# Background jobs of the opening feed-forward group of a hybrid encoder layer: weight sums begun two blocks earlier, both jobs stepped in each cell of the down-projections

## The chip, the cores and the metric

The kernel runs on one core of one Trainium2 chip. It is written with its own instruction order on TensorE, ScalarE, VectorE and GpSimd (in the feed-forward part the program text is the order); the order of SyncE's queue, which issues most of the transfers, is set by a scheduler. The metric is the time of one execution on the device, in microseconds. A profile of one execution gives the busy time of each engine (PE is TensorE's matrix multiplication, PEld its weight loads, DVE is VectorE, ACT is ScalarE, POOL is GpSimd, SP is SyncE), what each instruction waited for, and when each transfer landed.

## The reference, cut to what matters

One inference step of one layer, over 2048 prompt tokens and 64 sample tokens (2112 together), model width 1024, feed-forward width 2816. The first half of the layer (modulated norm, input projection, pooling mixer beside an mLSTM, output projection) isn't touched by the change. The second half is:

```python
    x = x + gt1 * mix
    h2 = rmsnorm(x, g2) * (1 + sc2) + sh2
    up = h2 @ w_up                                    # 1024 -> 2 * 2816
    upp = jnp.concatenate([conv_buf.astype(up.dtype), up], 1)
    conv = b_conv + sum(w_conv[j] * upp[:, j:j + T] for j in range(CONV_W))   # causal, width 3
    a, g = jnp.split(conv, 2, -1)
    x = x + gt2 * ((jax.nn.silu(g) * a) @ w_down)     # 2816 -> 1024
    ...
    y = rmsnorm(x, g_final)
```

All of it is float32.

## The kernel before, in words

**Arithmetic.** A float32 operand is split into a rounded high part and the low rest, and every product of the reference is computed as three matrix multiplications of such parts (`PASSES`). Splitting a weight tile takes a rounding on ScalarE (L411) and a subtraction on VectorE (L414).

**Groups, blocks, parts.** The 2112 tokens of the feed-forward part are done in three groups of 704 (`FT`; its half, 352, is `FH`). In each group the width 2816 is done in 22 blocks of 128 + 128 columns of `w_up` (one half for `a`, one for `g`). A block, `Pair.products`, multiplies the normed input of the group with its columns by a fast scheme of seven products in place of eight; each product (`product`, L1586) is 12 matmuls of 128 x 128 by 128 x 352. One of the seven, named T4, is not done in its own block but in the middle of the next one (`last_product`). The right-hand operands of the products are seven sums of chunks of the normed input, named B11, B21, B22, T1, T2, T3, T4; they come ready from the device's memory (`Bd`) and are held in SBUF as `hx`. Between its products a block steps along the convolution and the gate of the block before and the one before that. The result of a block is kept as `av` (a pool with 7 buffers, `AVB`).

In group 0 the 22 blocks come in four parts: 0 to 4, 5 to 9, 10 to 15 and 16 to 21. Behind each part stands the down-projection of what the part has made: for each of the 8 rows n of 128 output columns (`KD`) and each block k of the part one *cell*, which multiplies an `av` with a weight tile for two ranges of tokens (448 and 256 wide, `ENDS`): 2 x 3 matmuls. With five blocks in a part that is 40 cells, with six 48. At a row's end VectorE adds its two PSUM banks to `x3`, the residual (`rows_add`, L2009). There are six banks, two to a row. The rows 0 to 2 are begun early and ended together, since the last blocks of a part are not ready at first; what the last block still has to do (its T4 product, the sums, the convolution, the gate) lies in a list `todo`, whose steps are taken one behind each cell. In groups 1 and 2 the first parts are done by another scheme (`quad_down`), which needs sums of the down-projection's weights.

**Background jobs.** Two jobs of group 0 make what group 1 needs. They are Python generators, and a call of `tick(i)` carries job i on by one `yield`, that is by one instruction or none, so the place of a call sets the instruction's place in the order of its engine.

Job 0 is `quad_sums` (L1643): the sums of the down-projection's weights. For each of 16 pieces it takes a buffer of the `av` pool (the tile is named `qs`), loads the piece on SyncE's queue (L1649), makes four subtractions or additions on VectorE (L1653 to L1659) and stores the piece to `dsum` on SyncE's queue (L1662). A piece has 13 yields, the job 208.

Job 1 is `prepare` (L818): the seven sums of group 1's normed input. After a broadcast of the norms' factors it does four chunks; each loads two rows of the residual (`x2d`) into two scratch tiles `fscr` (L828, SyncE's queue), rescales them (`normed`, L737 on VectorE and L740 on ScalarE), and makes the seven sums from them, each with its high part (ScalarE, L788), its low part (VectorE, L774) and a store to `Bd` (L840, ScalarE's queue), between which VectorE makes the next difference (L770). The scratch pool has four buffers. The job has about 91 yields. When it has ended, a `reload` (L1872) loads the seven sums back into `hx`, on SyncE's queue, stepped by `tick(1)` too.

Calls of `tick` stand in these places: `product` makes two `tick(0)`, so a block with seven products makes 14; `products` makes four `tick(1)` (L1729, L1740, L1743, L1746); a cell of a down-projection does a step of `todo` if there is one, and else one `tick`, of job 1 or job 0 by turns (L2171). Job 0 gets `quad_sums` when the blocks of part 0 are done (L2137), job 1 gets `prepare` at the same place. Ahead of the last down-projection of the group whatever is left of both is run out at once (`drain`, L2140).

**Weights.** The tiles of `w_up` and `w_down` come as a stream: `pump` (L421) is called ahead of each product and behind each cell; it issues the loads on SyncE's queue, a few tiles ahead, into 5 raw buffers, and splits those next in line into 7 split buffers, so that the place of `pump` in the text sets where the splits stand in ScalarE's and VectorE's order.

The steps that the prediction speaks of are so on these engines: SyncE (loads of weights, of `x2d` and of the pieces, stores of pieces, reloads), ScalarE (roundings L411 and L788, the stores of `Bd`), VectorE (L414, L737, L770, L774, L1653 to L1659, L2009), TensorE (products L1594, cells L2160).

Of the kernel before, what the change touches and what calls it, by code (L numbers as in the profile page):

```python
# [64 lines left out]
def tile_layer(ctx: ExitStack, tc: tile.TileContext, xT, vecs, cst, rst, w_mod, w_ada, w_qkou, w_v, w_pool,  # L65
# [38 lines left out]
    bg = ([], [], [], [], [])  # L104

    def tick(i=0):
        q = bg[i]
        while q:
            try:
                next(q[0])  # L110
                return
            except StopIteration:
                q.pop(0)
# [143 lines left out]
    for g in range(NG):  # L257
        o = Grp()
# [400 lines left out]
    for g in range(NFG):  # L659
        o = Grp()  # L660
# [878 lines left out]
    def do(n=1):  # L1539

        for _ in range(n):
            if todo:
                todo.pop(0)()
# [91 lines left out]
    def give(bk):  # L1635
        used.remove(bk)
        free.append(bk)
# [49 lines left out]
    class Pair:  # L1687
# [10 lines left out]
        def products(self, old):  # L1698


            o, Bo, f = self.o, self.Bo, self.f
            self.before = old
            older = old and old.before
            if older and older.ended:
                older = None
            open_ = old and not old.shut

            def rest(*steps):
                for pair, step in steps:
                    if pair:  # L1710
                        step(pair)
            b1 = self.b1 = take()
            product(b1, Bo, "B11", True)
            if open_:
                old.sum_g1()
                old.sum_a()
            rest((older, Pair.gate))
            b2 = self.b2 = take(True)
            seed(b2, b1)
            rest((older, Pair.step_2))  # L1720
            b3 = self.b3 = take()
            product(b3, Bo, "T1", True)
            self.s5 = half_tile("s5")
            act.activation(self.s5, b3.t[:, :FH], AF.Copy)
            rest((old, Pair.scale_a), (older, Pair.step_3))
            if open_:
                old.last_product()
            rest((old, Pair.taps_a), (older, Pair.step_4))
            tick(1)  # L1729
            product(b1, Bo, "T2", False)  # L1730
            seed(b3, b1)
            if open_:
                old.sum_g0()
            rest((old, Pair.scale_g))
            self.ea = ext_tile(o, f, "a")
            product(b2, Bo, "B21", False)
            copied(o, 0, self.ea, b2)
            give(b2)
            rest((older, Pair.step_5), (old, Pair.taps_g))
            tick(1)  # L1740
            product(b1, Bo, "B22", False)
            rest((old, Pair.silu), (older, Pair.step_6))
            tick(1)  # L1743
            product(b3, Bo, "T3", False)
            rest((older, Pair.step_7))
            tick(1)  # L1746
            if older:
                older.ended = True

# [361 lines left out]
    for o in fgroups:  # L2111
        Bo = B[o.g]
        held = None
        for pi, part in enumerate(PARTS[o.g]):
            f0, f1_ = part
            nf = f1_ - f0
            lastp = pi == len(PARTS[o.g]) - 1
            ends = o.last and lastp
            av = [None] * nf
            quad = Quad() if paired(o.g, part) else None  # L2120
            if pi == 0:
                pair = None
            for f in range(f0, f1_):
                old, pair = pair, Pair(o, Bo, f, f - f0, av, quad)
                pair.products(old)
                if o.g == 0 and len(x3) < KD or pi == 0 and not bg[0]:
                    x3 += load_x2(o, range(len(x3), min(len(x3) + 2, KD)))
                if held is not None:
                    quad_down(o, held, pair, old)
                    held = None  # L2130
            if pi == 0 and o.g > 0:
                drain(0)
                x3 += load_x2(o, range(len(x3), KD))
            if not o.last:
                if pi == 0:
                    if o.g == 0:
                        bg[0].append(quad_sums())  # L2137
                    bg[1].append(prepare(fgroups[o.g + 1], fscr))
                if lastp:
                    drain(0, 1)  # L2140
                    B.append(Sums())
                    bg[1].append(reload(B[-1]))
            if lastp:
                ssum = fscr("ssum")
            if quad is not None:
                held = quad
                continue

            def down(bks, W, ks, secs, stays=False, plain=False):

                cells = [(i, k) for i in range(len(secs)) for k in ks]
                if plain:
                    cells.sort(key=lambda c: c[1])
                for c, (i, k) in enumerate(cells):
                    U = W.at(k // 4)
                    lo, hi = secs[i]
                    if k == 0:
                        bks[i].start(hi - lo)
                    for (a, b) in PASSES:
                        pe.matmul(bks[i].t[:, :hi - lo], U[:, a, k % 4 * P:(k % 4 + 1) * P], av[k][:, b, lo:hi],  # L2160
                                  start=(k == 0 and (a, b) == PASSES[0]), stop=(k == nf - 1 and (a, b) == PASSES[-1]))
                    if (k % 4 == 3 or k == nf - 1) and not stays and i == len(secs) - 1:
                        live[0] -= 1
                    if c % len(secs):
                        continue
                    pump()
                    settle()
                    if todo:
                        do()
                    else:  # L2170
                        tick(1 - c // len(secs) % 2)  # L2171

            def down_end(n, bks, secs):
                for bk, (lo, hi) in zip(bks, secs):
                    rows_add(o, n, lo, hi, bk)
                    give(bk)
                if not lastp:
                    return
                lo, hi = secs[0][0], secs[-1][1]
                if ends and n == KD - 1:  # L2180
                    sq7 = fscr()
                    for (a, b, s) in o.segs:
                        a, b = max(a, lo), min(b, hi)
                        if a < b:
                            act.activation(sq7[:, a - lo:b - lo], x3[n][:, a:b], AF.Square)
                    sums.append((sq7, lo))
                else:
                    fsq_acc(ssum, x3[n][:, lo:hi], lo, hi, n == 0)
                if ends:
                    act.activation(x3[n][:, lo:hi], x3[n][:, lo:hi], AF.Copy, scale=V[:, V_GF + n:V_GF + n + 1])  # L2190

            Ws = [Row() for _ in range(NE)]
            bks = []

            old = pair.before
            todo.extend([both_of(pair.sum_g1, old.gate), both_of(pair.sum_a, old.split_hi), both_of(old.split_lo, pair.scale_a)])
            for n in range(NE - 1):
                bks.append([take() for _ in ENDS])
                down(bks[n], Ws[n], range(nf - 2), ENDS, plain=n == 0)
                if n == 0:  # L2200
                    do(9)
                    pair.last_product()
                    todo.extend([both_of(pair.sum_g0, pair.scale_g), pair.taps_a, pair.taps_g, pair.silu, pair.gate,
                                 pair.split_hi, pair.split_lo])
            for n in range(NE - 1):
                down(bks[n], Ws[n], [nf - 2], ENDS)
            bks.append([take() for _ in ENDS])
            down(bks[-1], Ws[-1], range(nf - 1), ENDS)
            do(9)
            for n in range(NE):  # L2210
                down(bks[n], Ws[n], [nf - 1], ENDS)
                down_end(n, bks[n], ENDS)
            rows = {n: Row() for n in range(NE, KD)}
            for secs in [(c,) for c in ENDS] if ends else (ENDS,):
                sums = [(ssum, 0)]
                for n in range(NE, KD):
                    ps = [take() for _ in secs]
                    down(ps, rows[n], range(nf), secs, ends)
                    down_end(n, ps, secs)
                if ends:  # L2220
                    bg[0].append(final_end(o, x3, sums, *secs[0]))
            pair = None
        if not o.last:
            drain(1)
            bg[0].append(final(o, x3, ssum))
            x3 = []
# [87 lines left out]
```

## Time and profile before

| what | value |
|---|---|
| time, median of 3 runs | 2173.13 us (2171.32 to 2175.94) |
| the profiled execution: its own time, its span | 2174.68 us, 2172.9 us |
| TensorE's granted clock in it | 0.998 |
| TensorE, matmuls | 2151.4 us, 99% of the span |
| VectorE | 1634.9 us, 75% |
| ScalarE | 1096.1 us, 50% |
| GpSimd | 258.4 us, 12% |
| transfers | 539.51 MB, 248 GB/s in the mean |
| group 0: blocks 0 to 4, down-projection of part 0 | to 858.45 us, to 899.34 us |
| part 1: blocks 5 to 9, its down-projection | to 967.70 us, to 1005.67 us |
| part 2: blocks 10 to 15, its down-projection | to 1088.0 us, to 1132.2 us |
| part 3: blocks 16 to 21, its down-projection | to 1213.9 us, to 1257.8 us |

How to read it: the span is the time from the first instruction to the last as the profiler saw it, and the execution's own time has a little around it. The busy times of the engines overlap each other; an engine that is 99% busy leaves room for a change of 1% at most, where it alone is looked at. Times in windows and timelines are counted from the start of the span. A row of a timeline has the time at which an instruction begins, how long it took, the engine, the line of the kernel, the operation, the tile that is written and those that are read, their shapes, and in brackets how long the engine had stood idle before and what ended that. A row of a window has its bounds, its length, the busy time and the number of instructions of PE, PEld, DVE, ACT and POOL, the granted clock, the busy share of the DMA engines, and GB/s.

### The profile page before, as it was taken

To read this page: it belongs to the slowest core of one execution; us is meant where nothing else is said; L and a number is where in the kernel's file an instruction comes from. 1 tells how busy PE (TensorE), PEld (TensorE's weight loads), DVE (VectorE), ACT (ScalarE), POOL (GpSimd) and SP (SyncE) were. 2 spreads that over 40 slices of the span, in tenths; PEclk is the share of its full clock that TensorE was granted. 3 is DMA by queue.
4 is the path that set the end of the run, shared out by engine and by line. 5 is a ranking of instruction groups with operands and counts; after the bars stand their busy time and mean duration, and the time that the engine had idled before them with its cause. 6 is when DMAs were issued, how large, how long until landed. Compare 5 with 4: busy or idle time off the path is not lost.

```text
span 2172.9 us, 38060 instructions
## 1 busy us (share of the span) xinstructions
PE 2151.4 (99%) x13553; PEld 2044.4 (94%) x13553; DVE 1634.9 (75%) x3040; ACT 1096.1 (50%) x2181; POOL 258.4 (12%) x475
## 2 busy tenths in 40 slices
PE   8999999999999999999999999999999999999998
PEld 7888888888899999999999999999999999999998
DVE  5878668667955778797967668888886597887874
ACT  4554335334333446464736445655655365565554
POOL 0010000001000201010101220100101321111112
PEclk9999999999999999999999999999999999999999
DMA  8987997987888477888967976666668675555542
GB/s 319 328 305 233 323 321 246 309 302 244 301 283 288 169 260 239 282 292 300 350 214 255 321 245 222 234 208 209 228 222 274 223 255 186 170 177 190 171 160 77
DMA packets 297351, 539.51 MB, mean 248 GB/s; under 512 B 25760, under 2 KB 114336, under 8 KB 297160
## 3 DMA queue, kind: packets, MB, share of 16 engines
q1 hardware_dynamic: 286568, 511.87, 69.6%
q10 hardware_dynamic: 10592, 25.20, 3.0%
q8 instruction: 107, 1.75, 0.3%
q14 instruction: 84, 0.69, 0.1%
HBM read 410.98 MB, written 125.98 MB: 247 GB/s over the span
## 4 chain that ended last, share of the span: by engine, by line
PE 85%; DMA 5%; DVE 5%; issue 2%; ACT 2%; SPq 0%; POOL 0%; DVEq 0%; ACTq 0%; POOLq 0%
PE mm L1594 34%; PE mm L478 22%; PE mm L2160 12%; PE mm L2037 8%; PE mm L1133 3%; DVE wt L414 1%; DMA wt<-wsum 1%; PE m L1323 1%; DMA hl_kept<-wt 1%; PE m L1308 1%; PE m L1343 1%; PE m L1345 1%; DVE tg L1572 1%; DMA raw<-w_qkou 0%; ACT wt L411 0%
## 5 line engine op out<-in xcount | busy, mean ns | idle before, releaser
L1594 PE MATMUL mm<-hx,wt 128*128 128x352 f32 x5544 | 885.9, 321 | 0.7 <-DVE wt L414 0.5
L1594 PEld LDWEIGHTS mm<-hx,wt 128*128 128x128 f32 x5544 | 878.7, 188 | 2.6 <-DVE wt L414 2.0
L478 PE MATMUL mm<-hl,wt 128*128 128x512 f32 (+2 forms) x1920 | 387.4, 357 | 0.0
L411 ACT ACTIVATE wt<-raw 128x512 fp32r<-128x512 f32 (+3 forms) x470 | 276.6, 597 | 177.6 <-PE mm L478 52.8
L478 PEld LDWEIGHTS mm<-hl,wt 128*128 128x128 f32 x1920 | 316.4, 189 | 47.7 <-issue 4.4
L414 DVE TENSOR_TENSOR wt<-raw,wt 128x512 fp32r<-128x512 f32 (+3 forms) x470 | 312.8, 672 | 61.9 <-ACT wt L411 61.7
L2160 PE MATMUL mm<-av,wt 128*128 128x448 f32 (+1 forms) x1632 | 262.7, 322 | 0.0
L2160 PEld LDWEIGHTS mm<-av,wt 128*128 128x128 f32 x1632 | 250.4, 188 | 11.1
L2009 DVE SCALAR_TENSOR_TENSOR x<-mm,MOD,x 128x352 f32<-128x352 f32 (+3 forms) x360 | 167.5, 505 | 77.7 <-PE mm L2160 64.3
L2037 PE MATMUL mm<-av,wt 128*128 128x352 f32 x1344 | 220.7, 323 | 1.9 <-DVE x L2009 0.7
L2037 PEld LDWEIGHTS mm<-av,wt 128*128 128x128 f32 x1344 | 215.4, 188 | 5.0 <-DVE ea L1603 3.0
L1641 ACT ACTIVATE mm<-mm 128x352 f32<-128x352 f32 x196 | 87.8, 448 | 233.7 <-PE mm L1594 177.1
L478 PE MATMUL mm<-mx,wt 128*128 128x512 f32 (+1 forms) x960 | 182.9, 352 | 0.3 <-DVE scr L250 0.3
L478 PEld LDWEIGHTS mm<-mx,wt 128*128 128x128 f32 x960 | 159.4, 188 | 23.0 <-PE mm L478 0.5
L1572 DVE SCALAR_TENSOR_TENSOR ta<-ea,V,ta 128x704 f32<-128x704 f32 (+1 forms) x132 | 125.7, 953 | 58.4 <-ACT ta L1567 54.4
L1572 DVE SCALAR_TENSOR_TENSOR tg<-eg,V,tg 128x704 f32<-128x704 f32 (+1 forms) x132 | 125.7, 952 | 56.8 <-ACT tg L1567 54.3
L414 DVE TENSOR_TENSOR wt<-wt 128x512 fp32r<-128x512 f32 x196 | 133.0, 685 | 12.8 <-ACT wt L411 12.7
L411 ACT ACTIVATE wt<-wt 128x512 fp32r<-128x512 f32 x196 | 119.2, 622 | 36.6 <-DMA wt<-wsum 35.7
L1550 POOL COPY ea<-UC 128x2 f32<-128x2 f32 x66 | 33.1, 501 | 506.2 <-DVE ta L1572 407.3
L1781 ACT ACTIVATE tg<-tg 128x704 f32<-128x704 f32 (+1 forms) x66 | 52.5, 795 | 71.8 <-DVE tg L1572 71.8
L1133 PE MATMUL mm<-wt,hl 128*128 128x256 f32 (+1 forms) x576 | 71.4, 284 | 0.0
L1133 PEld LDWEIGHTS mm<-wt,hl 128*128 128x128 f32 x576 | 70.4, 190 | 0.8 <-issue 0.6
(305 smaller groups left out, 2207.0 us busy)
## 6 DMA issues: line engine op xcount, KB each, us to landing
wt<-wsplit SPq DMA_DIRECT2D x132, 512.0 KB, 4.3
raw<-w_up SPq DMA_DIRECT2D x198, 256.0 KB, 3.8
wt<-hl_kept SPq DMA_DIRECT2D x96, 512.0 KB, 6.3
wt<-wsum SPq DMA_DIRECT2D x132, 256.0 KB, 5.0
wsplit<-wt SPq DMA_DIRECT2D x66, 512.0 KB, 5.1
w<-w_up SPq DMA_DIRECT2D x88, 256.0 KB, 4.4
wsum<-w SPq DMA_DIRECT2D x44, 512.0 KB, 5.9
Bd<-fscr ACTq DMA_DIRECT2D x56, 352.0 KB, 4.3
```

The source lines that it names most:

```text
L411: act.activation(u.w[:, 0, :u.n], u.raw[:, :u.n], AF.Copy)
L414: dve.tensor_tensor(out=u.w[:, 1, :u.n], in0=u.raw[:, :u.n], in1=u.w[:, 0, :u.n].bitcast(F32), op=ALU.subtract)
L478: pe.matmul(ps[bi][:, :hi - lo], U[:, a, k % 4 * P:(k % 4 + 1) * P], mv[k][:, b, lo:hi], start=(at == 0 and pi == 0), stop=(k == order[-1] ...
L1133: pe.matmul(ps[ti][:n, :cols], h[4 * kh + k4][:, b, lo:lo + n], U[:, a, k4 % 2 * cols:(k4 % 2 + 1) * cols], start=(kh == 0 and k4 == 0 and ...
L1550: pool.tensor_copy(ext[:, 0:2], UC[:, f, :])
L1572: dve.scalar_tensor_tensor(out=t[:, :E], in0=ext[:, j:j + E], scalar=wc(j, f), in1=t[:, :E], op0=ALU.mult, op1=ALU.add)
L1594: pe.matmul(bk.t[:, :FH], U[:, a, kc * P:(kc + 1) * P], Bo.at(nm, kc, b), start=(first and kc == 0 and pi == 0), stop=(kc == 3 and pi == 2 ...
L1641: act.activation(to.t[:, :FH], bk.t[:, :FH], AF.Copy)
L1781: act.activation(self.tg[:, :E], self.tg[:, :E], AF.Silu)
L2009: dve.scalar_tensor_tensor(out=x3[n][:, a:b], in0=bk.t[:, a - lo:b - lo], scalar=gt2(n, s), in1=x3[n][:, a:b], op0=ALU.mult, op1=ALU.add)
L2037: pe.matmul(bk.t[:, :FH], U[:, a, c:c + P], quad.put(op, m, b), start=(first and m == 0 and pi == 0), stop=(m == 1 and pi == 2), skip_grou ...
L2160: pe.matmul(bks[i].t[:, :hi - lo], U[:, a, k % 4 * P:(k % 4 + 1) * P], av[k][:, b, lo:hi], start=(k == 0 and (a, b) == PASSES[0]), stop=(k ...
```

## The change

Three edits, all in the feed-forward part, and all acting in group 0 alone.

- In a block of group 0 the fourth `tick(1)` falls away, so job 1 is stepped three times in a block and not four times. In groups 1 and 2 nothing changes.
- `quad_sums` is given to job 0 right behind the products of block 2, and no longer behind the blocks of part 0, so that the blocks 3 and 4 step it too.
- In the down-projections of group 0 a cell that has no step of `todo` left steps both jobs, first job 0 and then job 1, where it stepped one of them by turns. This holds for the last down-projection of the group too, in which job 1 is the reload.

```diff
--- before.py
+++ after.py
@@ -1743,7 +1743,8 @@
             tick(1)
             product(b3, Bo, "T3", False)
             rest((older, Pair.step_7))
-            tick(1)
+            if o.g:
+                tick(1)
             if older:
                 older.ended = True
 
@@ -2123,6 +2124,8 @@
             for f in range(f0, f1_):
                 old, pair = pair, Pair(o, Bo, f, f - f0, av, quad)
                 pair.products(old)
+                if o.g == 0 and f == 2:
+                    bg[0].append(quad_sums())
                 if o.g == 0 and len(x3) < KD or pi == 0 and not bg[0]:
                     x3 += load_x2(o, range(len(x3), min(len(x3) + 2, KD)))
                 if held is not None:
@@ -2133,8 +2136,6 @@
                 x3 += load_x2(o, range(len(x3), KD))
             if not o.last:
                 if pi == 0:
-                    if o.g == 0:
-                        bg[0].append(quad_sums())
                     bg[1].append(prepare(fgroups[o.g + 1], fscr))
                 if lastp:
                     drain(0, 1)
@@ -2167,6 +2168,9 @@
                     settle()
                     if todo:
                         do()
+                    elif o.g == 0:
+                        tick(0)
+                        tick(1)
                     else:
                         tick(1 - c // len(secs) % 2)
 
```

## The prediction

> **What bounds the kernel now.** I read the page's sums first, then the windows of busy time over the opening feed-forward group, then the chain of waits there, then the timelines of VectorE and ScalarE at the end of one down-projection, and last the landing times of three kinds of transfers.
>
> ```profile
> span 2172.9 us, 38060 instructions
> PE 2151.4 (99%) x13553; PEld 2044.4 (94%) x13553; DVE 1634.9 (75%) x3040; ACT 1096.1 (50%) x2181; POOL 258.4 (12%) x475
> ```
>
> TensorE is the bound: time is lost only where it pauses. The group touched runs from 794 to 1258 us. In the windows below (bounds, length, then busy time of PE, PEld, DVE, ACT, POOL) the first two are blocks 3 and 4; the others run by turns over the down-projections of parts 0 and 1 and the blocks of parts 1 and 2.
>
> ```profile
> 831.00:844.60 13.60, 13.60 (x88) 13.60 (x87) 11.28 (x17) 9.84 (x18) 2.37 (x5) 1.00 0.76 252
> 844.60:858.40 13.80, 13.80 (x89) 13.80 (x88) 11.00 (x17) 9.55 (x18) 2.29 (x4) 1.00 0.55 197
> ...
> 858.45:899.34 40.89, 40.89 (x258) 39.19 (x257) 32.23 (x60) 16.63 (x33) 0.68 (x4) 1.00 0.61 189
> 899.34:967.70 68.36, 67.93 (x426) 66.94 (x425) 58.76 (x97) 46.12 (x84) 7.65 (x16) 1.00 0.96 352
> 967.70:1005.67 37.97, 37.87 (x238) 36.15 (x237) 29.39 (x56) 14.82 (x29) 1.24 (x4) 1.00 0.71 235
> 1005.67:1088.00 82.33, 82.12 (x517) 81.35 (x516) 73.53 (x124) 55.56 (x101) 10.74 (x20) 1.00 0.97 339
> ```
>
> PE is short of these windows by 0.43, 0.10 and 0.21 us, 0.74 together, and of no other. The pauses end in TensorE's timeline on a weight split of VectorE (L414):
>
> ```profile
> 947.62 17.51 PE L1594 MATMUL mm<-hx,wt 128*128 128x352 f32 x106 [0.29 <-DVE wt L414]
> ...
> 1067.01 17.31 PE L1594 MATMUL mm<-hx,wt 128*128 128x352 f32 x106 [0.21 <-DVE wt L414]
> ```
>
> Each matmul is drawn 322 ns long, but 264 of them pass in 41.99 us (0.159 each, next fence), so up to 0.16 us of each pause is hidden. With five pauses at most, 0.74 + 5 x 0.16 is about 1.5 us: all that this group can give back. The change can hardly win; the question is what it can lose.
>
> **The change part by part.** The chain of waits gives TensorE's pace and the starts of the stages:
>
> ```profile
> 858.45 2.91 PE mm L2160 x18
> ...
> 899.34 15.21 PE mm L1594 x96
> ...
> 1005.67 33.81 PE mm L1594 x214
> ...
> 1090.16 41.99 PE mm L2160 x264
> ```
>
> A product of 12 matmuls is 12 x 0.159 = 1.91 us, a cell of a down-projection (6 matmuls, after which the background jobs are stepped) 0.95 us.
>
> (1) The weight sums start behind block 2, not behind block 4. Blocks 3 and 4 get 28 calls of the job; 13 calls make one tile with four subtractions.
>
> ```profile
> L1653 DVE TENSOR_TENSOR qs<-qs x16: 416/419/426, 881.8 to 1135.7; 128x256 f32<-128x256 f32 x16
> ...
> sum 341.50, DVE 26.95; mean DVE 2.69
> ...
> sum 341.50, PE 0.80 PEld 0.69 DVE 31.71 ACT 21.55 POOL 0.00; mean PE 0.08 PEld 0.07 DVE 3.17 ACT 2.15 POOL 0.00
> ```
>
> (The sums are VectorE's time in the tiles qs and fscr over the windows of the group.) The weight sums cost VectorE 26.95 us in 208 calls, 0.13 a call, so blocks 3 and 4 get 28 x 0.13 = 3.6 us; VectorE idles 2.3 + 2.8 = 5.1 us there. Cost 0; without that cover, up to 3.6. SP gets two loads and a store more in these blocks, with the DMA engines at 0.76 and 0.55: cost 0. The job then ends in block 13 instead of block 17, which frees VectorE of about 4 x 14 x 0.13 = 7 us between blocks 13 and 17, where one of the pauses above sits (1067).
>
> (2) One step fewer of the preparation job per block: 31.71 us over 91 calls is 0.35 a call, so 1.7 us less VectorE work in blocks 5 to 9. Gain: part of the pauses. Of the 1.5 us I take 1.
>
> (3) In each row of the down-projections both jobs are stepped in every cell. Of 40 cells 10 are taken by the leftovers of the last block; the other 30 gave 11 calls to the sums and 19 to the preparation, and now give 30 to each. VectorE gets 19 x 0.13 + 11 x 0.35 = 6.4 us more: 32.23 becomes 38.6 of 40.9, and 29.39 becomes 35.8 of 38.0. It still fits. But the preparation isn't only work, it is a chain of transfers, and it is here that I expect the loss.
>
> The preparation splits seven sums per chunk: a rounding on ScalarE (L788), a subtraction on VectorE (L774), a store Bd from ScalarE's queue (L840). Its scratch tile `fscr` has four buffers, two of which hold the chunk, so sum n+2 waits until the store of sum n has landed. ScalarE before, in the down-projection of part 0:
>
> ```profile
> 887.19 0.33 ACTq L840 DMA_DIRECT2D Bd<-fscr  x1
> 887.56 0.50 ACT L788 ACTIVATE fscr<-fscr 128x352 fp32r<-128x352 f32 x1 [1.79 <-DVE fscr L774]
> ...
> 891.01 0.33 ACTq L840 DMA_DIRECT2D Bd<-fscr  x1
> 891.41 0.50 ACT L788 ACTIVATE fscr<-fscr 128x352 fp32r<-128x352 f32 x1 [0.40 <-DMA Bd<-fscr]
> ...
> 894.68 0.35 ACTq L840 DMA_DIRECT2D Bd<-fscr  x1
> 896.13 0.50 ACT L788 ACTIVATE fscr<-fscr 128x352 fp32r<-128x352 f32 x1 [0.88 <-DMA Bd<-fscr]
> ...
> 901.71 0.50 ACT L788 ACTIVATE fscr<-fscr 128x352 fp32r<-128x352 f32 x1 [2.05 <-DMA Bd<-fscr]
> ```
>
> Three roundings in a row already wait for landings: 887.19 to 891.4, 891.01 to 896.1, 894.68 to 901.7, that is 4.2, 5.1 and 7.0 us. With a step in every cell the whole chunk falls into cells 20 to 33, and the next chunk's loads (`fscr<-x2d`, L828) into cell 37. In the built program the first of these loads waits on SP for the fifth store (T2), whose buffer it takes; its rescaling (L737) then stands on VectorE ahead of the evictions of row 7, one subtraction of the weight sums and the split of the weights of block 5's fourth product. VectorE runs in order, so TensorE waits for this chain: store B11, landing, rounding and subtraction of T1, store, landing, the same for T2, landing, load, landing, rescaling, evictions, weight split. Its rows on VectorE:
>
> ```profile
> 880.34 0.48 DVE L2009 SCALAR_TENSOR_TENSOR x<-mm,MOD,x 128x256 f32<-128x256 f32 x1 [1.08 <-PE mm L2160]
> 880.74 0.28 DVE L414 TENSOR_TENSOR wt<-raw,wt 128x128 fp32r<-128x128 f32 x1
> 880.94 0.95 DVE L737 SCALAR_TENSOR_TENSOR fscr<-fscr,G,rb 128x704 f32<-128x704 f32 x1
> ...
> 886.64 0.52 DVE L774 TENSOR_TENSOR fscr<-fscr 128x352 fp32r<-128x352 f32 x1
> ...
> 983.54 1.07 DVE L2009 SCALAR_TENSOR_TENSOR x<-mm,MOD,x 128x448 f32<-128x448 f32 x2
> ...
> 989.67 0.68 DVE L2009 SCALAR_TENSOR_TENSOR x<-mm,MOD,x 128x448 f32<-128x448 f32 x1 [0.59 <-PE mm L2160]
> ```
>
> Start: VectorE reaches the subtraction of B11 after the evictions of row 3, which TensorE releases at 880.34: 880.34 + 0.48 + 0.28 + 0.52 is 881.6 at the earliest; with ScalarE's two rescalings ahead of the rounding I take 882.5. Twice rounding and subtraction, 0.50 + 0.52, and the queue's 0.1: 2.2. Tail: 0.95 + 1.07 + 0.42 + 0.68, less overlaps of 0.3: 2.8. Block 5 starts at 899.34, its fourth product is due at 899.34 + 3 x 1.91 = 905.1. So three landings of Bd plus one of x2d may take 905.1 - 882.5 - 2.2 - 2.8 = 17.6 us. Landings, first all of Bd in 880 to 909, then in 977 to 1006, then all of x2d:
>
> ```profile
> L840 ACTq DMA_DIRECT2D Bd<-fscr x6: 326/326/353, 887.2 to 908.6; - x6
> DMA to landing us min/median/max: 4.2/5.7/7.0
> ...
> L840 ACTq DMA_DIRECT2D Bd<-fscr x5: 326/326/327, 978.6 to 1002.5; - x5
> DMA to landing us min/median/max: 2.2/4.2/5.7
> ...
> L828 SPq DMA_DIRECT2D fscr<-x2d x8: 319/422/714, 872.3 to 1051.3; - x8
> DMA to landing us min/median/max: 5.8/6.0/8.2
> ```
>
> The three measured in a row (4.2 + 5.1 + 7.0) plus 6.0 are 22.3: 4.7 us late. Medians give 3 x 5.7 + 6.0 = 23.1: 5.5 late. The ends: 3 x 2.2 + 5.8 = 12.4, not late; 3 x 7.0 + 8.2 = 29.2, 11.6 late. I take 4.5, nearest to the three that stood in this place.
>
> The down-projection of part 1 repeats it one cell earlier, with chunk 2 and the loads of chunk 3, and now both rescalings stand ahead of the split. Start: the evictions of row 2 end at 984.6 (the row at 983.54), then about 5 us of splits, two rescalings and the evictions of row 3: 989.5. Budget to 1005.67 + 5.73 = 1011.4: 1011.4 - 989.5 - 2.2 - 3.7 = 16.0. Landings 3 x 4.2 + 5.8 = 18.4: 2.4 late. Ends: 12.4, not late; 3 x 5.7 + 8.2 = 25.3, 9.3 late. I take 2, because a VectorE held back once has a lighter backlog the second time.
>
> Queues: SP waits in that first load until about 900; behind it stand loads for block 6, due at 912.8, which SP before also issued around 900: cost 0, by the slack of 6 us over a landing. The evictions of rows 5 to 7 come up to 8 us late, but six PSUM banks, two a row, give two rows (9.5 us) of slack. POOL's order doesn't change. In the last down-projection the reload of the next group's operand is stepped faster, which moves it ahead of one weight load by eight issues; that weight is due in the last 2 us of the stage: cost 0, up to 1 if it lands late. TensorE's four small matmuls of the preparation move by a cell: 0.
>
> A fixed cost per transfer from a page would have it otherwise. By the Trainium skill, page "DMA: Bandwidth & Descriptors", section "Anatomy of one DMA — SWDGE (gpsimd) path", a transfer takes about 2.0 us plus its bytes over 436 GB/s, fitted on another issue path than this one; for 352 KB I estimate 2.8 us, a chain of 11.3, and no loss at all. The trace disagrees: only its shortest landings (2.2) are that short, the medians here are 4.2 to 6.0.
>
> Sum, on the profiled execution's 2174.68 us (span 2172.9 and 1.8 around it): + 4.5 + 2 - 1 = + 5.5, 2180.2. The median of the runs is 2173.13, 1.55 below that execution, so I forecast 2178.6.
>
> **The rivals.** *Not slower: the transfers stay hidden.* If the landings of Bd stay under (17.6 - 6.0) / 3 = 3.9 us in part 0 and 3.4 in part 1, both chains end in time and only the pauses go: up to - 1.5, 2171.6. For it: two of the five landings in part 1 were near 2.2, and the DMA engines are only 0.61 and 0.71 busy in these stages. Against it: no landing in part 0 was below 4.2. One chain late by less than 4 us belongs here too: 2172 to 2177.
> The other two rest on VectorE's evictions in the down-projection of part 0 (group of instructions: busy time and mean ns, then idle time before them and what ended it) and on one block's window of part 2, TensorE never short in it:
>
> ```profile
> L2009 DVE SCALAR_TENSOR_TENSOR x<-mm,MOD,x 128x448 f32<-128x448 f32 (+1 forms) x15 | 8.6, 587 | 4.7 <-PE mm L2160 4.6
> ...
> 1046.30:1059.80 13.50, 13.50 (x87) 13.50 (x86) 12.22 (x21) 10.05 (x18) 1.19 (x4) 1.00 1.01 362
> ```
>
> *VectorE becomes the bound in the down-projections.* At 38.6 of 40.9 us any wait of VectorE has no cover; it idled 4.7 us for evictions alone, which cannot be filled. Then about 2 us more are lost in each of the two, 2182.6. For it: the waits for ScalarE's roundings come on top. Against: banks and weights run two rows ahead.
> *Early weight sums hold up blocks 3 and 4.* 3.6 us in 5.1 us of idle time that is scattered: up to 2 us, 2180.6 on top of the main case. Against: no PE pause shows in blocks where VectorE is busy 12.2 of 13.5.
> *Faster.* It would take more than 4.3 us of removed pauses, where the group has 1.5.
>
> **How the numbers follow.** A measurement here tells about 0.2% from no change, 4.3 us. Main case (both chains late) with the two slower rivals: 0.57, 2177.5 to 2186. Chains hidden or nearly so: 0.39, 2171 to 2177.5. Faster: 0.04. The range for 8 in 10 takes in the hidden case without its last tenth and the main case up to 11 us late less the gain: 2171.4 to 2185. The main case alone: 2177 to 2185.
>
> **What would show it.** Right: in block 5 VectorE idle for 3 us and more before L737, ended by the landing of fscr<-x2d, and then TensorE waiting for wt L414 near 905; the same, smaller, near 1011; ScalarE's waits for Bd landings several times as long as before in both down-projections; the pause at 1067 gone, the weight sums ended in block 13. Wrong: L737 starting without such a wait, or the fourth products of blocks 5 and 10 on time; or pauses in blocks 3 and 4.

## The result

The changed kernel takes 2191.74 us in the median of six runs (2187.99 to 2194.71), the kernel before 2173.26 us in the same comparison: 18.5 us slower by the medians, a ratio of 1.0083 with a 95% interval of 1.0069 to 1.0097. The direction was forecast, the size was not: 5.5 us stood in the sum, and 2191.7 lies above the range.

The page's first lines of the changed kernel answer to those of before; the engines do the same work in 16 us more:

```profile
span 2189.2 us, 38057 instructions
PE 2158.1 (99%) x13553; PEld 2051.5 (94%) x13553; DVE 1633.4 (75%) x3040; ACT 1095.4 (50%) x2181; POOL 256.9 (12%) x475
```

All of the loss lies in the opening group: it began at 791.90 and its last down-projection ended at 1273.85, 481.95 us against 463.80 before (794.01 to 1257.81), 18.2 more. TensorE's timeline shows where (start, busy time, engine, line, tiles, and in brackets how long it had stood idle and what ended that):

```profile
907.64 6.67 PE L1594 MATMUL mm<-hx,wt 128*128 128x352 f32 x25 [4.40 <-DVE wt L414]
...
974.52 2.74 PE L2161 MATMUL mm<-av,wt 128*128 128x448 f32 x16 [1.44 <-DVE wt L414]
977.65 0.56 PE L1594 MATMUL mm<-hx,wt 128*128 128x352 f32 x2 [0.39 <-DVE eg L1603]
...
1023.61 6.65 PE L1594 MATMUL mm<-hx,wt 128*128 128x352 f32 x25 [4.43 <-ACT mm L1641]
```

With the 0.16 us that the drawn length of a matmul hides, the two long pauses are 4.56 and 4.59 us. The windows of the changed kernel (bounds, length, busy time of PE, PEld, DVE, ACT and POOL, then the granted clock, the DMA engines' share and GB/s) show what stands behind them:

```profile
902.92:907.64 4.72, 0.32 (x3) 0.03 (x2) 2.93 (x6) 2.77 (x6) 0.00 (x0) 0.83 0.96 381
907.64:912.60 4.96, 4.96 (x17) 4.96 (x18) 2.61 (x4) 1.92 (x4) 0.00 (x0) 0.50 0.84 260
...
925.00:940.00 15.00, 15.00 (x92) 15.00 (x92) 12.83 (x21) 10.93 (x20) 2.29 (x4) 1.00 0.91 305
...
990.00:1013.00 23.00, 23.00 (x144) 22.04 (x143) 18.67 (x42) 8.22 (x19) 0.00 (x0) 1.00 0.79 260
...
1023.61:1028.60 4.99, 4.99 (x17) 4.99 (x18) 3.92 (x9) 3.11 (x6) 0.00 (x0) 0.50 0.83 311
```

After each long pause the granted clock is 0.50 for 5 us, and 17 matmuls take 0.293 us each where they took 0.159: 17 x 0.134 is 2.3 us more, twice. The Trainium skill, page "TensorE: Matmul & The Clock Gate", section "What's actually happening", says that an idle window of about 3.4 us halves the array's clock and that a busy one of that length frees it again; these two pauses, longer than that, agree with it; what shorter ones do is told at the end.

The ledger of the group: two long pauses, 9.15; half clock behind them, 4.6; three shorter pauses (0.8 at 954, then 1.6 and 0.55 in the rows above), 3.0; a slower pitch from 912 to 975 with the clock given as full (92 matmuls in 15.00 us, two of them at the edges: 0.167 each and not 0.159), 2.9; less the pauses of before, which are gone, 2.0 (1.5 us of pauses, and 0.5 us in the slower matmul behind each). That makes 17.6 of the 18.2; the rest isn't placed.

What TensorE waited for, on VectorE and then in SyncE's queue, in the changed kernel:

```profile
904.71 0.95 DVE L737 SCALAR_TENSOR_TENSOR fscr<-fscr,G,rb 128x704 f32<-128x704 f32 x1 [4.85 <-DMA fscr<-x2d]
905.58 1.07 DVE L2010 SCALAR_TENSOR_TENSOR x<-mm,MOD,x 128x448 f32<-128x448 f32 x2
906.56 0.41 DVE L1659 TENSOR_TENSOR qs<-qs 128x256 f32<-128x256 f32 x1
906.89 0.69 DVE L414 TENSOR_TENSOR wt<-raw,wt 128x512 fp32r<-128x512 f32 x1
...
1021.34 1.98 DVE L737 SCALAR_TENSOR_TENSOR fscr<-fscr,G,rb 128x704 f32<-128x704 f32 x2 [5.59 <-DMA fscr<-x2d]
```

```profile
895.31 0.56 SPq L1649 DMA_DIRECT2D qs<-w_quad  x1
895.96 1.12 SPq L398 DMA_DIRECT2D wt<-wsum  x2
897.18 1.13 SPq L828 DMA_DIRECT2D fscr<-x2d  x2
...
1012.46 0.57 SPq L1662 DMA_DIRECT2D dsum<-qs  x1
1013.15 0.64 SPq L398 DMA_DIRECT2D wt<-wsum  x1
1013.90 2.79 SPq L828 DMA_DIRECT2D fscr<-x2d  x2
```

The rescaling of the next chunk waits for its load. At the first long pause the evictions, a subtraction of the weight sums and the split for which TensorE waits stand behind it in VectorE's order: the order that the prediction gave. The second long pause ends otherwise. TensorE stops two products into block 10, for a copy on ScalarE (L1641), and ahead of that copy ScalarE has its own part of the rescaling (L740), which waits for VectorE's:

```profile
1022.32 0.88 ACT L740 ACTIVATE fscr<-fscr,MOD 128x704 f32<-128x704 f32 x1 [6.63 <-DVE fscr L737]
1023.11 0.45 ACT L1641 ACTIVATE mm<-mm 128x352 f32<-128x352 f32 x1
```

The loads went out at 897.18 and 1013.90, and the chain of waits has their landings:

```profile
897.18 7.43 DMA fscr<-x2d
```

```profile
1013.90 7.42 DMA fscr<-x2d
```

(one row from each of the two stretches). The stores of the sums, and who waited for them, over the first of the two down-projections, as one tile's summary:

```profile
L840 ACTq DMA_DIRECT2D Bd<-fscr x7: 326/326/349, 881.3 to 896.5; - x7
...
  ACT fscr L788: 9.0, 4
...
DMA to landing us min/median/max: 2.5/4.5/7.1
```

So ScalarE did wait for landings, 9.0 us there and 8.8 us in the second. The third pause, at 973, has the same form with the other job: a piece of the weight sums is loaded and VectorE waits for it, ahead of a weight split.

```profile
970.70 0.43 DVE L1653 TENSOR_TENSOR qs<-qs 128x256 f32<-128x256 f32 x1 [2.27 <-DMA qs<-w_quad]
```

### The profile page after: what moved, and what is told of

It is laid out like the page before. It is cut to its first block, busy times and chain, and to the rows that moved or that the text cites. A ratio compares the mean times of both kernels' runs of the same rounds, so it can differ in the third digit from the quotient of the medians.

```text
span 2189.2 us, 38057 instructions
## 1 busy us (share of the span) xinstructions
PE 2158.1 (99%) x13553; PEld 2051.5 (94%) x13553; DVE 1633.4 (75%) x3040; ACT 1095.4 (50%) x2181; POOL 256.9 (12%) x475
## 4 chain that ended last, share of the span: by engine, by line
PE 84%; DVE 6%; DMA 5%; issue 2%; ACT 2%; SPq 1%; POOL 0%; DVEq 0%; POOLq 0%; ACTq 0%
PE mm L1594 34%; PE mm L478 23%; PE mm L2161 10%; PE mm L2038 8%; PE mm L1133 3%; DVE wt L414 2%; DMA hl_kept<-wt 1%; PE m L1323 1%; DMA fscr<-x2d 1%; DMA wt<-wsum 1%; PE m L1343 1%; PE m L1345 1%; PE m L1308 1%; DVE tg L1572 1%; DVE x L2010 1%
## 5 line engine op out<-in xcount | busy, mean ns | idle before, releaser
L1594 PE MATMUL mm<-hx,wt 128*128 128x352 f32 x5544 | 893.6, 323 | 10.3 <-DVE wt L414 5.5
L1594 PEld LDWEIGHTS mm<-hx,wt 128*128 128x128 f32 x5544 | 886.4, 189 | 12.2 <-DVE wt L414 6.8
L414 DVE TENSOR_TENSOR wt<-raw,wt 128x512 fp32r<-128x512 f32 (+3 forms) x470 | 312.2, 671 | 65.4 <-ACT wt L411 65.0
L1641 ACT ACTIVATE mm<-mm 128x352 f32<-128x352 f32 x196 | 87.8, 448 | 243.5 <-PE mm L1594 186.6
L414 DVE TENSOR_TENSOR wt<-wt 128x512 fp32r<-128x512 f32 x196 | 132.1, 682 | 11.0 <-ACT wt L411 10.9
```

Of the source, the lines that this page charges most:

```text
L414: dve.tensor_tensor(out=u.w[:, 1, :u.n], in0=u.raw[:, :u.n], in1=u.w[:, 0, :u.n].bitcast(F32), op=ALU.subtract)
L1594: pe.matmul(bk.t[:, :FH], U[:, a, kc * P:(kc + 1) * P], Bo.at(nm, kc, b), start=(first and kc == 0 and pi == 0), stop=(kc == 3 and pi == 2 ...
L1641: act.activation(to.t[:, :FH], bk.t[:, :FH], AF.Copy)
```

## The experiments

Theories at the start: *chain* (the preparation, at the pace of the cells, ends late at the end of a down-projection, and VectorE's fixed order passes that on to TensorE), *sums* (the weight sums at that pace do it) and *load* (VectorE's extra work does it). All ratios are to the kernel before.

### The third edit alone

```diff
                     if todo:
                         do()
+                    elif o.g == 0:
+                        tick(0)
+                        tick(1)
                     else:
```

> Only the third edit: both jobs in every cell of group 0's down-projections; the weight sums start behind part 0's blocks and a block keeps four steps of the preparation. Chain theory (the preparation at the pace of the cells puts the rescaling of a chunk two cells behind its loads, at the end of a down-projection; VectorE waits there, TensorE behind it, and after a pause of 4.6 us TensorE runs some 16 matmuls at half clock): the wait near 905 us is there as in the changed kernel, about 4.6 + 2.4 us; in part 1 the loads come in cell 31 and not 36, so that wait shrinks to between 0 and 4 us. In all 7 to 12 us slower than before. Sums theory (the weight sums at the pace of the cells hold up SyncE's queue and VectorE): 14 to 18 us slower, as in the changed kernel. Load theory (VectorE's 6.4 us of extra work in each down-projection): 14 to 18 us slower too, in many small pauses.

Measured: 1.0061 (1.0046 to 1.0076), 13 us slower; pauses of 3.4 us near 908 and of 2.7 us near 1017, each with half clock soon behind it. The third edit alone makes most of the loss; the number lies just above what the chain theory allowed and just below the others', so it doesn't choose between them.

### The first two edits alone

```diff
                     if todo:
                         do()
-                    elif o.g == 0:
-                        tick(0)
-                        tick(1)
                     else:
```

> The first two edits without the third: weight sums from block 2 on, three steps of the preparation in a block, the cells step the jobs by turns as before. Chain theory: no wait near 905; the loads of chunk 2 fall into cell 34 of part 1's down-projection and its rescaling into cell 37, so a short pause of 0 to 2 us near block 10; in all between 1.5 us faster and 2 us slower than before. Sums theory: the early start alone loads SyncE in blocks 3 and 4: 0 to 4 us slower. Load theory: between 1.5 us faster and 1 us slower.

Measured: 1.0001 (0.9991 to 1.0011). No pause stands near 905; the longest of the group is 0.5 us. The early start of the weight sums and the step left out of each block cost nothing that can be measured, and bring next to nothing: the group takes 462.95 us where it took 463.80, as other pauses, 0.9 us in all, stand in place of those of before.

### One job at the pace of the cells, the other by turns

The changed kernel with the preparation in every second cell:

```diff
                     elif o.g == 0:
                         tick(0)
-                        tick(1)
+                        if lastp or c // len(secs) % 2 == 0:
+                            tick(1)
```

> The changed kernel, but in the cells of parts 0 to 2 only the weight sums are stepped each time; the preparation every second time. Chain theory: no wait near 905, chunk 2 as in the kernel without the third edit: between 1 us faster and 3 us slower than before. Sums theory: 14 to 18 us slower. Load theory: the sums are 2.5 of the 6.4 us more work, so 5 to 8 us slower.

and with the weight sums in every second cell:

```diff
                     elif o.g == 0:
-                        tick(0)
+                        if c // len(secs) % 2:
+                            tick(0)
                         tick(1)
```

> The changed kernel, but in the cells only the preparation is stepped each time; the weight sums every second time. Chain theory: both long waits of the changed kernel stay, near 905 and 1020, each 4 to 5 us with half clock behind it: 12 to 17 us slower than before. Sums theory: between 1 us faster and 3 us slower. Load theory: 9 to 12 us slower.

Measured: with the preparation by turns 1.0021 (1.0009 to 1.0033), 4.6 us; with the sums by turns 1.0062 (1.0047 to 1.0077), 13.5 us. The two long waits need the preparation at the pace of the cells. TensorE in the kernel with the sums by turns, its timeline and then two windows:

```profile
907.93 2.33 PE L1594 MATMUL mm<-hx,wt 128*128 128x352 f32 x13 [2.45 <-DVE wt L414]
...
1014.64 4.54 PE L1594 MATMUL mm<-hx,wt 128*128 128x352 f32 x17 [3.19 <-ACT mm L1641]
```

```profile
907.90:912.90 5.00, 4.97 (x31) 4.98 (x32) 4.97 (x10) 3.38 (x7) 0.00 (x0) 1.00 0.83 285
...
1015.40:1018.60 3.20, 3.20 (x12) 3.20 (x12) 3.13 (x8) 1.89 (x5) 0.00 (x0) 0.50 0.53 191
```

Both waits are there, shorter (2.6 and 3.4 us), and only the second has half clock behind it, here for 3.2 us. In that run the slower pitch of 0.167 us holds from 1019 to 1094.

The load theory gave 5 to 8 and 9 to 12, in many small pauses. Both intervals still touch these numbers, but the traces show few long pauses and not many small ones, so it falls. The kernel with the preparation by turns did a little worse than the chain theory had it, by one pause of 3.4 us near 950 with half clock behind it. VectorE there:

```profile
949.63 0.43 DVE L1653 TENSOR_TENSOR qs<-qs 128x256 f32<-128x256 f32 x1 [3.72 <-DMA qs<-w_quad]
```

This load went out at 941.57 and landed 8.03 us later; the five steps between a load and its first subtraction give it some 5 us. The weight sums cost by the same rule: a landing that the steps leave too little time for, on an engine that works in order.

### The rescaling later

The changed kernel, with the rescaling moved away from its load:

```diff
-            for _ in range(2):
+            for _ in range(8 if kc else 2):
                 yield
```

> The changed kernel, but from the second chunk on eight steps and not two lie between a chunk's loads and its rescaling; every load keeps its place, the rescalings of chunks 1 and 2 move from cells 39 and 38 to block 6 and to later cells. Chain theory, now with three measured runs behind it: the two long waits go and their half clock with them, 14 us; what stays are the pauses on the first subtraction of a piece of the weight sums (0.9, 1.7 and 0.6 us in the changed kernel): between 1 us faster and 4 us slower than before. If instead it is the mere pace of both jobs that costs (VectorE's work, SyncE's queue), the time stays 14 to 18 us above before.

and, with it, the first subtraction of the weight sums:

```diff
                 nc.sync.dma_start(out=w, in_=w_quad[d, :, :, c:c + 256])
-                for _ in range(5):
+                for _ in range(9):
                     yield
                 ...
                 nc.sync.dma_start(out=dsum[d, :, :, c:c + 256], in_=w)
                 yield
-                yield
-                yield
```

> As the kernel with late rescaling, and nine steps in place of five between the load of a piece of the weight sums and its first subtraction (two fewer behind its store). Chain theory, taken to both jobs (VectorE, in its fixed order, waits for a landing that the steps leave too little time for): the pauses on the weight sums go too, between 1.5 us faster and 1.5 us slower than before. If pace alone costs: 14 to 18 us slower.

Measured: 1.0142 (1.0125 to 1.0159) and 1.0096 (1.0081 to 1.0111), 31 and 21 us slower: a clear miss. Part of it is the edit's own fault: it also delays the preparation of group 2, which is then not done when group 1's last down-projection begins and is run out at once, a pause of 12 us near 1684 in the first kernel and near 1671 in the second. In group 0 the second kernel takes only 3.8 us more than the kernel before, the first 15.5 us. So the time for the weight sums takes most of the loss there, too. What is left in the first is instructive. The six steps push the sums of chunk 2 into the last rows of part 1's down-projection, and there they stop TensorE without any rescaling. Rows of the chain of waits of the first of the two kernels, in order of time:

```profile
1008.58 6.19 DMA Bd<-fscr
...
1014.79 0.51 ACT fscr L788
...
1015.32 0.54 DVE fscr L774
...
1015.88 7.50 DMA Bd<-fscr
...
1023.40 0.50 ACT fscr L788
1023.89 0.36 ACT mm L1641
```

A store lands, the next sum is rounded and subtracted, it is stored and lands, and ScalarE, waiting for that landing, holds up the copy (L1641) for which TensorE stands 5.2 us near 1019. So it isn't the distance between load and rescaling alone: any link of the chain that falls to the end of a down-projection stops an engine that the next block needs.

### What a pause costs

The kernel before, with additions on VectorE ahead of the fourth product of six blocks:

```diff
+PADS = {(0, 17): 2, (0, 19): 3, (0, 21): 4, (1, 17): 5, (1, 19): 6, (1, 21): 8}
...
             tick(1)
+            if (o.g, f) in PADS:
+                pad = fscr()
+                dve.memset(pad, 0.0)
+                for _ in range(PADS[o.g, f]):
+                    dve.tensor_tensor(out=pad, in0=pad, in1=pad, op=ALU.add)
             product(b1, Bo, "T2", False)
```

> The kernel before with 2, 3 and 4 additions of 0.9 us put on VectorE ahead of the fourth product of blocks 17, 19 and 21 of group 0, and 5, 6 and 8 in the same blocks of group 1; nothing else. It measures what a pause of TensorE costs beyond itself. If the half clock is set off by the length of the pause alone, matmuls behind pauses under some length between 1.7 and 2.7 us keep their pitch of 0.159 us, and behind longer ones run at 0.293 for 1.2 to 2.5 us of extra time each. If it belongs to the waits of the changed kernel, none of the pauses shows it. In all 10 to 25 us slower than before.

Measured, in one run: 2202.48 us, 27 us above before. Four of its pauses, and the windows behind them (one line is added, so L1595 and L415 are L1594 and L414):

```profile
1183.93 6.29 PE L1595 MATMUL mm<-hx,wt 128*128 128x352 f32 x38 [1.56 <-DVE wt L415]
...
1213.30 5.34 PE L1595 MATMUL mm<-hx,wt 128*128 128x352 f32 x22 [2.49 <-DVE wt L415]
...
1621.05 7.26 PE L1595 MATMUL mm<-hx,wt 128*128 128x352 f32 x28 [4.83 <-DVE wt L415]
...
1652.92 7.34 PE L1595 MATMUL mm<-hx,wt 128*128 128x352 f32 x34 [2.44 <-DVE wt L415]
```

```profile
1183.90:1188.90 5.00, 4.97 (x31) 4.97 (x32) 4.79 (x8) 1.84 (x3) 0.49 (x1) 1.00 0.42 149
...
1213.20:1216.90 3.70, 3.60 (x13) 3.61 (x14) 3.66 (x6) 1.18 (x2) 0.49 (x1) 0.56 1.06 404
...
1621.00:1626.30 5.30, 5.25 (x18) 5.23 (x19) 5.23 (x10) 1.81 (x3) 0.32 (x1) 0.50 0.31 109
...
1653.80:1657.30 3.50, 3.50 (x14) 3.22 (x13) 3.16 (x6) 1.31 (x2) 0.32 (x1) 0.52 0.34 126
```

A pause of 1.7 us leaves the clock alone; 2.65 and 2.6 us set off some 3.4 us of half clock (1.5 us lost each, at the second about a microsecond after work has begun again); 5.0 us sets off more than 5 us of it (2.5 lost). The half clock follows a pause of TensorE as such, whether a landing or additions on VectorE made it.

### More room for the chain, more time for the sums

Five scratch buffers and not four:

```diff
-        return spare[0].tile([P, FT], dt, tag="fscr", name="fscr", bufs=4)
+        return spare[0].tile([P, FT], dt, tag="fscr", name="fscr", bufs=5)
```

> The changed kernel with five scratch buffers fscr in place of four (the room comes from the tile of the convolution's last rows, which in the last group takes a scratch buffer). Every instruction keeps its place; only the sums' buffers come free sooner. Landing theory (the preparation is a chain: with four buffers, two of them held by the chunk, each sum waits for the landing of the second last; that chain ends too late at the end of a down-projection): one landing of 4 to 5 us leaves each chain, the two long waits of 4.6 us fall to 0 to 2 us, without half clock; in all between 0 and 6 us slower than before. Distance theory (two cells between a chunk's loads and its rescaling, against a landing of 7 us, whatever the buffers): both waits stay, 13 to 18 us slower.

Measured: 1.0063 (1.0049 to 1.0077), 13.6 us slower; the waits shrink from 4.6 to 3.0 and 2.0 us, each still with half clock behind it, and the one behind a load of the weight sums, near 973, grows from 1.6 to 2.6 us, now with half clock too. By its number this is the distance theory's; the trace says what held the loads instead. SyncE's queue (the diff moves the lines by two: L1651 loads a piece of the weight sums, L1664 stores it):

```profile
898.52 0.55 SPq L1651 DMA_DIRECT2D qs<-w_quad  x1
899.16 1.07 SPq L398 DMA_DIRECT2D wt<-wsum  x2
900.29 1.01 SPq L828 DMA_DIRECT2D fscr<-x2d  x2
...
1012.68 0.57 SPq L1664 DMA_DIRECT2D dsum<-qs  x1
1013.36 0.58 SPq L398 DMA_DIRECT2D wt<-wsum  x1
1014.58 1.83 SPq L828 DMA_DIRECT2D fscr<-x2d  x2
```

The loads of the next chunk go out right behind transfers of the weight sums, as they do in the changed kernel, and those wait themselves: the first for an earlier piece's store to land, the second for VectorE's subtraction. Two things can hold the loads, the chain of landings and this queue, and with five buffers the queue is left. Hence two more kernels, both with nine steps ahead of the first subtraction (the second diff of the section on the rescaling), which changes where these transfers stand: one with five buffers, one with four.

> The changed kernel with both: five scratch buffers, and nine steps between the load of a piece and its first subtraction. Landing theory: all pauses of the changed kernel go or shrink under 1 us each: between 1.5 us faster and 3 us slower than before. Distance theory: 11 to 15 us slower, since only the pauses on the weight sums, 3 us, go.

> The changed kernel with nine steps and not five between the load of a piece of the weight sums and its first subtraction (two fewer behind its store), and four scratch buffers as it had. The kernel with five buffers and nine steps lost about 4 us, the one with five buffers and five steps about 14; in that one the preparation's landings were in time, and the loads of the next chunk stood on SyncE's queue behind a transfer of the weight sums. Two-limits theory (the chain of landings and that queue each hold the loads back by themselves): with four buffers the landings hold them again, the loads go out near 896 and 1004 or later, TensorE pauses 2 to 4.5 us near both: 8 to 15 us slower than before. Queue theory (only the transfers of the weight sums ahead of the loads matter): as with five buffers, 2 to 6 us slower.

Measured: with five buffers 1.0019 (1.0009 to 1.0029), 3.9 us; with four 1.0027 (1.0017 to 1.0038), 5.6 us. With neither edit it was 18.5, with five buffers alone 13.6. The time for the weight sums is worth 10 to 13 us, the fifth buffer 2 to 5. The two-limits theory had 8 to 15 for four buffers: it named the places and the issue times (899.0 and 1004.6), but the pauses were 1.4 and 1.3 us. VectorE in the kernel with four buffers and nine steps:

```profile
904.37 0.95 DVE L737 SCALAR_TENSOR_TENSOR fscr<-fscr,G,rb 128x704 f32<-128x704 f32 x1 [2.90 <-DMA fscr<-x2d]
```

It still waits for the load, but the load landed in 5.3 us where it took 7.4 in the changed kernel, with no load of the weight sums right ahead of it. Whether the landing is shorter for that reason wasn't tried by itself.

Last, the milder form of the change: the preparation by turns, the weight sums in each cell, and nine steps.

> The kernel with the preparation stepped in every second cell and the weight sums in each, with nine steps and not five between the load of a piece of the weight sums and its first subtraction (two fewer behind its store). Its forerunner lost 5.0 us at 950, where VectorE waited 3.7 us for the landing of such a load (8.0 us). Landing theory: that wait goes and no other comes: between 1.5 us faster and 1.5 us slower than before. Theory that the pace of the weight sums costs by VectorE's work: still 3 to 5 us slower.

Measured: 1.0003 (0.9995 to 1.0012). Both jobs run without a loss in time, with one pause of 1.1 us left near 903, and nothing is gained, as the 2 us of pauses before let one expect. No kernel here beats the one before.

## Why the prediction was right, and where it was wrong

*Gain.* At most 1.5 us of pauses were to go, 1 was taken; they went, and with the slower matmul behind each 2.0 us. The kernel with the first two edits alone shows that nothing larger was to be had.

*Parts 1 and 2 at cost 0.* Right, by the same kernel.

*VectorE's work in the down-projections at cost 0, and the rival that makes it the bound.* Right and wrong in that order: from 990 to 1013 TensorE is busy 23.00 of 23.00 us. (19 x 0.13 + 11 x 0.35 is 6.3 and not 6.4 us.)

*The first chain: 4.5 us predicted, 4.56 measured.* The place, the order on VectorE and the size came out, the size partly by luck. Counted from the start of block 5, the fifth store landed (at 896.1) 2.7 us sooner than the three measured landings gave; the load then left about a microsecond later than its buffer allowed, behind a weight sum's load and two weight loads in SyncE's queue, and took 7.4 us to land, not 6.0. These errors, -2.7, +1.1 and +1.4, cancel.

*The second chain: 2 us predicted, 4.59 measured.* The term was too small, and its path was another. The chain started at the time forecast (16.2 us ahead of block 10), but the load landed in 7.4 us, not 5.8, again behind a transfer of the weight sums; and TensorE was held by ScalarE's copy two products into block 10, 1.9 us before the fourth product was due, for which the sum had waited. The pause ends on L1641, not on wt L414. The discount for a lighter backlog had no ground.

*What a pause costs.* This is the step that failed: the sum took a pause of 4.5 us as 4.5 us lost. The granted clock halves behind it, which makes 4.6 us more for the two. In the windows that it read no pause was longer than 0.5 us, but ahead of the feed-forward part the trace of before shows it, where TensorE stood 1.9 us and then ran at half clock:

```profile
438.03 1.65 PE L1323 MATMUL m<-va,kw 128*128 128x129 f32 x8 [1.85 <-DVE kw L250]
```

```profile
438.48:441.89 3.41, 3.41 (x13) 2.95 (x12) 3.31 (x9) 0.00 (x0) 0.00 (x0) 0.50 1.06 407
```

The page of the Trainium skill named above has the rule too, and the prediction did not weigh it.

*Queues at cost 0.* This step failed too. The weight sums' transfers on SyncE and their loads' landings were costed at nothing. They made the two pauses at 973 to 978, 2.2 us (the one of 0.8 us near 954 has no such wait: there VectorE is busy with the preparation ahead of the split). And with nine steps for them and the same four buffers the two long pauses shrink from 4.6 to 1.4 and 1.3 us, without half clock, and 5.6 of the 18.5 us are left. So the greater part of those two hangs on them as well, and four buffers alone do not make 4.5 us of pause. That the first term met its measurement was luck in this, too.

*Left over.* The slower pitch, 2.9 us, was in nobody's list. With these, 5.5 + 4.6 + 2.6 + 3.0 + 2.9 - 1.0 is 17.6, where 2.6 is what the second chain had too little and 1.0 what went beyond the gain taken.

*The fixed cost per transfer.* The estimate by the Trainium skill's page "DMA: Bandwidth & Descriptors", section "Anatomy of one DMA — SWDGE (gpsimd) path", would have had no loss. The runs disagree as the trace of before did: 352 KB landed in 2.5 us at best, 4.5 in the median and 7 to 8 at the end of a down-projection, where the DMA engines are over 0.9 busy.

Left open: what makes the slower pitch; and how the wait would divide between buffer and queue if the order of SyncE's queue alone were changed, which wasn't tried.

## What to carry to other kernels

A background job that is stepped along with the main work keeps its transfers covered only as long as the steps between an issue and its first use last longer than the landing: stepping it twice as fast halves that cover, for each link of a chain and for whatever stands behind it in the same queue. Look at what the in-order engine does next after such a use; at the seam to a stage that needs fresh weights every 1.9 us it has nothing to spare. And reckon with half clock behind a pause of TensorE of about 2 us or more: it cost 1.2 to 2.9 us on top of the pause here, though some pauses of 2.1 to 2.6 us had none.

## What was not expected of the hardware

The half clock sets in after less idle time than the 3.4 us of the Trainium skill's page named above: pauses of 2.6 and 2.65 us set it off where VectorE was padded, and one of 2.0 us in the kernel with five buffers and five steps, while one of 2.6 us with the sums by turns did not. The length of the pause doesn't decide; where it lies on a fixed grid does. In every trace here the granted clock changes only at whole multiples of 3.413 us from its first change, so half clock holds for 3.41 us or a multiple of it; this bears out the free-running window of that page of the Trainium skill. In the changed kernel it holds from 906.00 to 912.83, and begins while TensorE still stands:

```profile
906.00:909.42 3.42, 1.78 (x6) 1.79 (x7) 3.42 (x7) 1.99 (x4) 0.00 (x0) 0.50 0.78 292
909.42:912.83 3.41, 3.41 (x14) 3.41 (x13) 0.84 (x3) 1.79 (x4) 0.00 (x0) 0.50 0.88 254
```

The pause of 2.0 us with five buffers lay whole in one window of the grid (1020.50 to 1023.91, TensorE busy 1.54 of 3.41 us), and the next window ran at half clock. The pause of 2.6 us with the sums by turns was cut by an edge (busy 2.81 us from 902.67 to 906.08, and 1.56 us from 906.08 to 909.49), and the clock stayed full. In the feed-forward parts of all runs each window at full clock with 2.06 us or more of idle TensorE was followed by half clock and none with under 1.85; of three with 1.85 to 1.89, one was. What decides between those isn't shown.

TensorE has two pitches at full granted clock for the same matmul, 0.159 and 0.167 us. The slower one holds for stretches of 10 to 80 us, in the kernel before too (from 794 to 805). Many of these stretches begin behind a pause or at the end of half clock and end at the seam of a stage, but with five buffers one begins near 1069 amid products, with no pause there. In the stretch from 925 to 946 the kernel before has 0.160 (133 matmuls in 21.00 us, two of them at the edges). What sets it is open.
